# An encoder layer's normalisation stage written out in each engine's order, with B's products ahead and the meta tokens second

## The chip, the cores and the metric

The kernel runs on one core of a Trainium2 chip. TensorE (PE) multiplies matrices; VectorE (DVE), ScalarE (ACT) and GpSimd (POOL) work element by element; SyncE (SP) issues most of the transfers (DMAs). Each of these engines runs its instructions strictly in order, and waits on semaphores for what other engines or transfers have yet to finish. The metric is the time of one launch on the device in microseconds (us), the median of three runs.

## The reference

The reference is one encoder layer in float32 on 512 tokens of 2048 values, with 16 learned meta tokens put ahead of them. Three branches (linear attention, differential attention, a state-space scan) read column groups of one input projection. What the change touches is the start:

```
h = jnp.concatenate([meta, x], axis=1)
u = rmsnorm(h, norm_w)
proj = u @ w_in.astype(dt_)
(gq, gk, gv, ggate, gcode, dq, dk, dv, dgate, z, xbc, dt_raw) = jnp.split(proj, split_idx, axis=-1)
...
dt = jax.nn.softplus(dt_raw.reshape(Bsz, L, 2, SSD_HEADS).astype(jnp.float32) + ssd_dt_bias.astype(jnp.float32))
```

Here rmsnorm divides each token by the root of its mean square and multiplies by norm_w.

## The kernel before

**Blocks.** The tokens lie in blocks of 128: t = 0 to 3 are x's, t = 4 is the 16 meta tokens. The first half of the columns (HA = 272) holds meta and blocks 0 and 1, the second (HB = 256) blocks 2 and 3. The 2048 values of a token are 16 tiles (KT) of 128, called features here and counted by k.

**The stage.** Each block of x is loaded in four tiles of 512 columns (line 86). `normalize` squares each tile with a running sum (ACT line 259, DVE line 262), adds the four sums and EPS (line 264), raises the result to −0.5 on POOL (line 266, "r", called the root here) and scales the tiles with it. `features` transposes 128 x 128 pieces on PE into a PSUM tile "pb" (line 279). ACT copies it, scaled by norm_w, into `uh[k]` (helper line 72), rounded to the part that TensorE takes in one pass. DVE writes what is left into `ul[k]` (line 282).

**The products.** A weight is split in the same way: ACT copies the raw tile "wraw" to "whi" (line 72), DVE subtracts to "wlo". For a column group "B", `t1_half` makes three products per feature: hi·uh, hi·ul, lo·uh (line 39, into a PSUM tile "pm"). For a small group "comb" (gcode and dt_raw, 64 columns whose hi and lo lie side by side) `comb_half` makes two. B's weights come from line 157 and are split in four pieces of 512 columns (line 162), comb's from line 228 in two (line 231). All later weights come through `wsplit` (load line 141, split line 146), in pieces of 1024 columns, under a high priority. Its raw tiles "wraw" share two buffers with B's.

**After the stage.** The first half of B is copied to "xp" (ACT), comb is transposed and goes into "dts", "dtt" and, with exp of A_log ("ea", line 358), into "at" (line 360).

**What sets the order.** The program is written block after block, and a scheduler in the framework decides where each instruction stands on its engine, by its own estimates. Semaphores are placed after that. The semaphores of SP's and ACT's transfers are eight, DMAHW0 to DMAHW7, used in turn: a transfer is issued only when the one that had the same semaphore eight issues earlier has landed. The small vectors come by lines 116 to 119, the meta tokens by line 107, the identity matrix that the transposes use by line 112, the norm weights "gn" of two branches by lines 304 and 305, scaled at once by lines 306 and 307.

Of the kernel before, what the change touches and what calls it, by code (L numbers as in the profile page):

```python
# [42 lines left out]
def encoder_kernel(ctx, tc, x, meta, rel_bias, final_norm_w, norm_w, w_in, w_out, gla_wa2, gla_ba,  # L43
                   gla_norm_w, diff_lambda, diff_norm_w, conv_w, conv_b, A_log, dt_bias, ssd_D,
                   ssd_norm_w, masks, umask, onehot, out):
    nc = tc.nc
# [36 lines left out]
    def load_x(t):
        for j in range(4):
            xt[t, j] = slot("ya" if t < 2 else "o", [P, 512], name="xt")
            nc.sync.dma_start(xt[t, j], xv[t][:, j * 512:(j + 1) * 512])

    warm = const.tile([P, 1], F32, name="warm")
    nc.vector.memset(warm, 0.0)
    nc.scalar.activation(warm, warm, AF.Exp)  # L90
# [34 lines left out]

# [26 lines left out]
    def t1_weights(c0, nk, tag):  # L152

        out_ = []
        for k0 in range(0, KT, 8):
            raw = wpool.tile([P, 8, P], F32, name="wraw")
            nc.sync.dma_start(raw, win[:, k0:k0 + 8, c0:c0 + P])
            for i in range(0, 8, nk):
                hi = slot(tag, [P, nk, P], F32R, name="whi")
                lo = slot(tag, [P, nk, P], F32R, name="wlo")  # L160
                cpy(hi, raw[:, i:i + nk])
                tt(lo, raw[:, i:i + nk], hi.bitcast(F32), ALU.subtract)
                out_.append((hi, lo))
        return out_

    def t1_half(acc, ws, hf):
        nk = KT // len(ws)
        o, us = (acc[0][:, 0:HA], slice(0, HA)) if hf == 0 else (acc[1][:, 0:HB], slice(HA, L))
        for k in range(KT):
            hi, lo = ws[k // nk]  # L170
            for n, (wt, ur) in enumerate(((hi, uh[k]), (hi, ul[k]), (lo, uh[k]))):
                mm(nc, o, wt[:, k % nk, :], ur[:, us], k == 0 and n == 0, k == KT - 1 and n == 2)
# [61 lines left out]
    load_x(2)  # L234
    load_x(3)

    def comb_half(acc, hf):

        o, us = (acc[0][:, 0:HA], slice(0, HA)) if hf == 0 else (acc[1][:, 0:HB], slice(HA, L))
        for k in range(KT):  # L240
            for n, ur in enumerate((uh[k], ul[k])):
                mm(nc, o, comb_w[k // 8][:, k % 8, :], ur[:, us], k == 0 and n == 0, k == KT - 1 and n == 1)

    vt = const.tile([P, 92], F32, name="vt")
    pv = pb()
    nc.tensor.transpose(pv[:, 0:92], vecs, ident[0:92, 0:92])
    nc.vector.tensor_copy(vt, pv[:, 0:92])
    nw = vt[:, 0:16]
    gba = vt[:, 88:92]

    def normalize(t):
        rows = NM if t == 4 else P
        ss = small.tile([P, 1], F32, name="ss")
        ssq = small.tile([P, 5], F32, name="ssq", bufs=5)
        nc.gpsimd.memset(ssq[:, 4:5], EPS)
        for j in range(4):
            scr = slot("w")
            if j < (2 if t < 2 else 3):
                nc.scalar.activation(scr[0:rows, 0:512], xt[t, j][0:rows], AF.Square, scale=D ** -0.5,
                                     accum_out=ssq[0:rows, j:j + 1])  # L260
            else:
                nc.vector.tensor_tensor_reduce(scr[0:rows, 0:512], xt[t, j][0:rows], xt[t, j][0:rows], 1.0 / D, 0.0,
                                               ALU.mult, ALU.add, ssq[0:rows, j:j + 1])
        nc.vector.tensor_reduce(ss[0:rows], ssq[0:rows], AX.X, ALU.add)
        r = small.tile([P, 1], F32, name="r")
        gtt(r[0:rows], ss[0:rows], mhalf[0:rows, 0:1], ALU.pow)
        for j in range(4):
            if j == 3:
                cpy(xt[t, j][0:rows], xt[t, j][0:rows], scale=r[0:rows, 0:1])
            else:  # L270
                ts_(xt[t, j][0:rows], xt[t, j][0:rows], r[0:rows, 0:1], None, ALU.mult)

    def features(parts, us):
        for k in range(KT):
            pt = pb()
            n = 0
            for t in parts:

                nc.tensor.transpose(pt[:, n:n + P], xt[t, k // 4][:, (k % 4) * P:(k % 4 + 1) * P], ident)
                n += NM if t == 4 else P  # L280
            cpy(uh[k][:, us], pt[:, 0:n], scale=nw[:, k:k + 1])
            stt(ul[k][:, us], pt[:, 0:n], nw[:, k:k + 1], uh[k][:, us].bitcast(F32), ALU.mult, ALU.subtract)
# [20 lines left out]
    gn = const.tile([P, 2, P], F32, name="gn")  # L303
    nc.sync.dma_start(gn[:, 0], gla_norm_w.broadcast_to([P, P]))
    nc.sync.dma_start(gn[:, 1], diff_norm_w.broadcast_to([P, P]))
    ts_(gn[:, 0], gn[:, 0], 0.5, None, ALU.mult)
    ts_(gn[:, 1], gn[:, 1], 1.0 - LAMBDA_INIT, 0.5, ALU.mult, ALU.mult)
# [701 lines left out]
```

## Time and profile before

| What | Value |
|---|---|
| Time, median of 3 runs | 900.89 us (899.99 to 901.36) |
| The profiled execution's own time | 897.21 us |
| Span of its records | 895.3 us |
| TensorE busy | 865.2 us, 97% of the span |
| VectorE, ScalarE, GpSimd busy | 536.1, 419.8, 142.2 us |

The span is what the profiler's records cover; the profiled execution's own time has 1.9 us around it. The rows below are times of that one execution, counted from the start of the span.

### The profile page before, as it was taken

What the parts mean: (1) busy time and instruction counts of PE and PEld (TensorE: products, weight loads), DVE (VectorE), ACT (ScalarE), POOL (GpSimd) and SP (SyncE); (2) the same over time, 40 slices, a digit from 0 to 9 for tenths busy, and PEclk for the clock granted to TensorE, in tenths of its full rate; (3) what the DMA queues carried; (4) which work ended last, traced back from release to release, by engine and by line L of the source; (5) the groups of instructions that cost most, each with busy time, mean ns of one, the idle gap of its engine ahead of it and who ended that gap; (6) DMA issues with size and microseconds to landing.
All of it is one profiled execution on the core that took longest, in us unless ns stands there. A gap on an engine that the chain in (4) does not pass through costs nothing.

```text
span 895.3 us, 14457 instructions
## 1 busy us (share of the span) xinstructions
PE 865.2 (97%) x5705; PEld 772.8 (86%) x5705; DVE 536.1 (60%) x1035; ACT 419.8 (47%) x828; POOL 142.2 (16%) x185
## 2 busy tenths in 40 slices
PE   3999989999999999999999999999999999999996
PEld 3999989998888899999999999988888888888884
DVE  6655897998977787944532577665552633232333
ACT  7667945439743487543222364543431432231322
POOL 2000004640335302000330000100110002020200
PEclk9999999999999999999999999999999999999998
DMA  9534731244523233222355322243223532222225
GB/s 240 135 94 129 205 94 49 71 119 142 158 78 94 72 94 95 72 71 72 90 148 141 95 75 82 86 118 116 71 84 96 169 133 94 94 94 95 82 83 188
DMA packets 104116, 96.77 MB, mean 108 GB/s; under 512 B 8624, under 2 KB 75816, under 8 KB 104048
## 3 DMA queue, kind: packets, MB, share of 16 engines
q1 hardware_dynamic: 99647, 85.43, 34.0%
q0 software_dynamic: 1520, 5.17, 2.0%
q10 hardware_dynamic: 2880, 5.24, 1.8%
q8 instruction: 45, 0.74, 0.3%
q14 instruction: 24, 0.19, 0.1%
HBM read 91.55 MB, written 6.41 MB: 109 GB/s over the span
## 4 chain that ended last, share of the span: by engine, by line
PE 76%; DVE 9%; ACT 5%; DMA 5%; issue 3%; SPq 1%; POOL 0%; ACTq 0%; POOLq 0%; DVEq 0%
PE pm L39 65%; PE pb L39 8%; DVE acc L410 2%; DMA xt<-in_x_dram 2%; ACT dtm L437 1%; DVE wlo L146 1%; DVE sg L446 1%; DMA sb<-xd 1%; ACT sg L445 1%; PE pb L894 1%; PE pb L848 1%; DVE m L551 1%; DMA sg<-xd 1%; ACT whi L72 1%; DMA wraw<-in_w_in_dram 1%
## 5 line engine op out<-in xcount | busy, mean ns | idle before, releaser
L146 DVE TENSOR_TENSOR wlo<-wraw,whi 128x1024 fp32r<-128x1024 f32 (+1 forms) x128 | 160.2, 1251 | 192.1 <-ACT whi L72 191.9
L72 ACT ACTIVATE whi<-wraw 128x1024 fp32r<-128x1024 f32 (+1 forms) x134 | 137.3, 1025 | 270.3 <-PE pm L39 214.5
L39 PE MATMUL pm<-uh,whi 128*128 128x272 f32 (+2 forms) x960 | 223.7, 298 | 2.6 <-ACT xp L72 2.6
L39 PE MATMUL pm<-ul,whi 128*128 128x272 f32 (+2 forms) x960 | 226.1, 299 | 0.0
L39 PE MATMUL pm<-uh,wlo 128*128 128x272 f32 (+2 forms) x928 | 216.5, 297 | 0.0
L39 PEld LDWEIGHTS pm<-uh,whi 128*128 128x128 f32 x960 | 155.4, 189 | 7.9 <-ACT xp L72 2.8
L39 PEld LDWEIGHTS pm<-ul,whi 128*128 128x128 f32 x960 | 155.4, 189 | 4.9 <-issue 0.4
L39 PEld LDWEIGHTS pm<-uh,wlo 128*128 128x128 f32 x928 | 150.1, 189 | 4.5
L39 PE MATMUL pm<-whi,mh 128*128 128x512 f32 x256 | 100.9, 394 | 0.4 <-ACT mh L72 0.4
L39 PE MATMUL pm<-whi,ml 128*128 128x512 f32 x256 | 101.0, 396 | 0.0
L39 PE MATMUL pm<-wlo,mh 128*128 128x512 f32 x256 | 100.9, 394 | 0.0
L39 PE MATMUL pm<-wlo,uh 128*128 128x512 f32 x256 | 100.9, 394 | 0.0
L39 PE MATMUL pm<-whi,ul 128*128 128x512 f32 x256 | 100.8, 395 | 0.0
L39 PE MATMUL pm<-whi,uh 128*128 128x512 f32 x256 | 100.1, 397 | 0.0
L129 POOL TENSOR_TENSOR rs_r<-rs_v,mhalf 128x1 f32<-128x1 f32 (+1 forms) x28 | 20.6, 737 | 266.1 <-DVE rs_v L128 194.1
L39 PEld LDWEIGHTS pm<-whi,mh 128*128 128x128 f32 x256 | 48.1, 188 | 11.6 <-ACT mh L72 0.6
L39 PEld LDWEIGHTS pm<-wlo,mh 128*128 128x128 f32 x256 | 48.1, 188 | 11.2
L39 PEld LDWEIGHTS pm<-whi,ul 128*128 128x128 f32 x256 | 48.1, 188 | 11.0
L39 PEld LDWEIGHTS pm<-whi,ml 128*128 128x128 f32 x256 | 48.0, 188 | 11.0
L39 PEld LDWEIGHTS pm<-wlo,uh 128*128 128x128 f32 x256 | 48.2, 188 | 10.5
L39 PEld LDWEIGHTS pm<-whi,uh 128*128 128x128 f32 x256 | 48.1, 188 | 10.4
L928 POOL TENSOR_TENSOR hx<-hx,fw 128x512 f32<-128x512 f32 x12 | 18.1, 1543 | 164.9 <-ACT junk L915 164.9
(299 smaller groups left out, 1160.7 us busy)
## 6 DMA issues: line engine op xcount, KB each, us to landing
wraw<-in_w_in_dram SPq DMA_DIRECT2D x96, 512.0 KB, 3.9
wraw<-in_w_out_dram SPq DMA_DIRECT2D x30, 512.0 KB, 3.6
xt<-in_x_dram SPq DMA_DIRECT2D x16, 256.0 KB, 4.9
sg<-xd SPq DMA_DIRECT2D x16, 256.0 KB, 4.4
sb<-xd SPq DMA_DIRECT2D x16, 256.0 KB, 4.8
hx<-in_x_dram ACTq DMA_DIRECT2D x16, 256.0 KB, 3.7
out_dram<-hx SPq DMA_DIRECT2D x16, 256.0 KB, 2.9
tabr<-tabd POOLq DMA_DIRECT2D x4, 520.0 KB, 6.9
```

The lines of the kernel that those rows point to most:

```text
L39: nc.tensor.matmul(out, lhsT=lhsT, rhs=rhs, start=start, stop=stop)
L72: nc.scalar.activation(out, in_, AF.Copy, **kw)
L129: gtt(r[0:rows, 0:cols], v[0:rows, 0:cols], mhalf[0:rows, 0:cols], ALU.pow)
L146: tt(lo, raw, hi.bitcast(F32), ALU.subtract)
L410: stt(acc, xp[:, k:k + L], cw[:, k:k + 1], acc, ALU.mult, ALU.add)
L437: nc.scalar.activation(dtm[:, c], mtile[:, M_LE, :], AF.Identity, scale=dtd[:, c, h:h + 1], bias=dtt[:, c, 16 + h:17 + h])
L445: nc.scalar.activation(sg[:, c], sg[:, c], AF.Identity, bias=Xs[:, 0, c, h:h + 1])
L446: stt(sg[:, c], sb[:, c], Xs[:, 1, c, h:h + 1], sg[:, c], ALU.subtract, ALU.min)
L551: tt(m, m, sc, ALU.mult)
L848: nc.tensor.transpose(pt[:, c * P:(c + 1) * P], w_[:, c * P:(c + 1) * P], ident)
L894: nc.tensor.transpose(pt[:, c * P:(c + 1) * P], src[:, j * P:(j + 1) * P], ident)
L928: gtt(hx[t, b], hx[t, b], fw[b], ALU.mult)
```

## The change

The whole stage is written out by hand, in the order in which each engine is to run it, inside `tc.manual_schedule()`, which leaves each engine's instructions in program order. The functions `load_x`, `t1_weights`, `comb_half`, `normalize` and `features` become smaller steps, and a loop over the features calls them. Block 0 is squared first, then the meta tokens, then block 1; block 1's root stands ahead of the meta tokens'. The identity and the meta tokens (now four transfers) are issued from ACT's queue, the small vectors from POOL's. The first half's loop makes B's products feature by feature, and those of comb 12 features later; two of 28 other steps (`todo`) stand behind each feature. The loads of block 2 come ahead of comb's weights. gn's load and scaling are written much later in the program, and "ea" keeps its place in the program's order.

```diff
@@ the start: loads, tiles, splits are taken out of their old places @@
-    for i in range(2):
-        mt = wpool.tile([P, 1024], F32, name="mt", tag="whi" if i else "wlo", bufs=3)
-        nc.gpsimd.memset(mt, 0.0)
-        nc.sync.dma_start(mt[0:NM], meta[:, i * 1024:(i + 1) * 1024])
...
-    for t in (4, 0, 1):
-        normalize(t)
-    features((4, 0, 1), slice(0, HA))
-    comb_ps, b_ps = (pm(), pm()), (pm(), pm())
-    t1_half(b_ps, b_w, 0)
-    comb_half(comb_ps, 0)
-    for t in (2, 3):
-        normalize(t)
-    features((2, 3), slice(HA, L))
-    t1_half(b_ps, b_w, 1)
-    comb_half(comb_ps, 1)
...
+    def turn(hf, k, parts):
+
+        if (hf, k) not in pts:
+            pts[hf, k] = pb()
+        n = 0
+        for t in BL[hf]:
+            if t in parts:
+
+                nc.tensor.transpose(pts[hf, k][:, n:n + P], xt[t, k // 4][:, (k % 4) * P:(k % 4 + 1) * P], ident)
+            n += NM if t == 4 else P
...
+    with tc.manual_schedule():
+
+        load_x(0)
+        nc.scalar.dma_start(ident, masks[M_ID])
+        nc.vector.memset(warm, 0.0)
+        nc.scalar.activation(warm, warm, AF.Exp)
+        for j in range(4):
+            xt[4, j] = slot("ya", [P, 512], name="mt")
+            nc.vector.memset(xt[4, j], 0.0)
+            nc.scalar.dma_start(xt[4, j][0:NM], meta[:, j * 512:(j + 1) * 512])
+        nc.vector.memset(zp, 0.0)
+        nc.gpsimd.memset(mhalf, -0.5)
+        load_x(1)
...
+        load_b()
+        load_b()
+        load_x(2)
+        load_comb()
+        load_comb()
+        load_x(3)
+        cpy(XE, zp[0:96, 0:8].rearrange("p a b -> p (a b)"))
+        cpy(BE, vz[0][0:96])
+        cpy(RB, vz[0][0:96, 0:4])
+
+        square(0, 0, "A")
+        square(0, 2, "V")
+        square(0, 1, "A")
+        square(0, 3, "V")
+        root(0)
...
+        for j in range(4):
+            square(4, j, "A")
...
+        square(1, 2, "V")
+        square(1, 0, "A")
+        square(1, 3, "V")
+        square(1, 1, "A")
+        root(1)
+        root(4)
+        scale(4, 0, "V")
+        scale(0, 1, "A")
+        split_b()
+        LEAD = 3
...
+        CLAG = 12
+        for k in range(KT + CLAG):
+            if k < KT:
+                parts_of_u(0, k)
+                if k + LEAD < KT:
+                    turn(0, k + LEAD, BL[0])
+                prod_b(0, k)
+            for _ in range(2):
+                if todo:
+                    todo.pop(0)()
+            if k >= CLAG:
+                prod_comb(0, k - CLAG)
+            if k >= KT + CLAG - LEAD:
+                turn(1, k - (KT + CLAG - LEAD), BL[1])
         for k in range(KT):
...
+            parts_of_u(1, k)
+            if k + LEAD < KT:
+                turn(1, k + LEAD, BL[1])
+            prod_b(1, k)
+            if k >= 1:
+                prod_comb(1, k - 1)
+        prod_comb(1, KT - 1)
...
-    nc.scalar.activation(ea, row32[:, 32:64], AF.Exp)
+    tc.keep_in_program_order(nc.scalar.activation(ea, row32[:, 32:64], AF.Exp))
...
+    nc.sync.dma_start(gn[:, 0], gla_norm_w.broadcast_to([P, P]))
+    nc.sync.dma_start(gn[:, 1], diff_norm_w.broadcast_to([P, P]))
+    tc.keep_in_program_order(ts_(gn[:, 0], gn[:, 0], 0.5, None, ALU.mult))
+    tc.keep_in_program_order(ts_(gn[:, 1], gn[:, 1], 1.0 - LAMBDA_INIT, 0.5, ALU.mult, ALU.mult))
```

What this makes of the engines' order is shown at three places. First the start of ACT, before; a row is a line, an operation, output<-input and size, and in brackets the semaphores that it waits for (DMAHW3 and so on are landings of transfers).

```order
L90 ACTIVATE warm<-warm 128x1 [waits DVE_49]
L72 ACTIVATE XE<-zp 96x512 [waits DVE_49]
L72 ACTIVATE BE<-zp 96x128
L72 ACTIVATE RB<-zp 96x4
L259 ACTIVATE w,ssq<-mt 16x512 [waits DMAHW3_49,Pool_49]
L259 ACTIVATE w,ssq<-mt 16x512
L259 ACTIVATE w,ssq<-mt 16x512 [waits DMAHW4_49,Pool_49]
L259 ACTIVATE w,ssq<-xt 128x512 [waits DMAHW0_49]
```

The same place after:

```order
L279 ACTIVATE warm<-warm 128x1 [waits DVE_49]
L283 DMA mt<-in_meta_tokens_dram 16x512 [waits DVE_49]
L283 DMA mt<-in_meta_tokens_dram 16x512 [waits DMAHW0_49,DVE_49]
L283 DMA mt<-in_meta_tokens_dram 16x512 [waits DMAHW2_49,DVE_49]
L283 DMA mt<-in_meta_tokens_dram 16x512 [waits DMAHW4_49,DVE_49]
L72 ACTIVATE XE<-zp 96x512 [waits DVE_49]
L72 ACTIVATE BE<-zp 96x128
L72 ACTIVATE RB<-zp 96x4
L186 ACTIVATE w,ssq<-xt 128x512 [waits DMAHW1_49]
L186 ACTIVATE w,ssq<-xt 128x512
```

Four issues now stand ahead of ACT's first copy and first square. DMAHW0 is here the landing of the identity, DMAHW1 to DMAHW4 those of block 0's four tiles.

Second, DVE around the first weight split of 1024 columns, before; ul_136 to ul_151 are the first half's ul of k = 0 to 15.

```order
L282 SCALAR_TENSOR_TENSOR ul_148<-pb,vt,uh_132 128x272
L282 SCALAR_TENSOR_TENSOR ul_149<-pb,vt,uh_133 128x272
L282 SCALAR_TENSOR_TENSOR ul_150<-pb,vt,uh_134 128x272
L146 TENSOR_TENSOR wlo<-wraw,whi 128x1024
L282 SCALAR_TENSOR_TENSOR ul_151<-pb,vt,uh_135 128x272
```

After, ul_99 to ul_114 are k = 0 to 15, and line 116 is the split:

```order
L259 SCALAR_TENSOR_TENSOR ul_108<-pb,vt,uh_92 128x272
L236 TENSOR_TENSOR whi<-wraw,whi 128x8x64
L116 TENSOR_TENSOR wlo<-wraw,whi 128x1024
L259 SCALAR_TENSOR_TENSOR ul_109<-pb,vt,uh_93 128x272
L189 ISA w,ssq<-xt 128x512
L189 ISA ssq 128x1
L259 SCALAR_TENSOR_TENSOR ul_110<-pb,vt,uh_94 128x272
L189 ISA w,ssq<-xt 128x512
L189 ISA ssq 128x1
L195 TENSOR_REDUCE ss<-ssq 128x1
L259 SCALAR_TENSOR_TENSOR ul_111<-pb,vt,uh_95 128x272
L205 TENSOR_SCALAR xt<-xt,r 128x512 x2
```

The split has moved from behind k = 14 to behind k = 9, and block 3's squares and scales from ahead of it to behind it. On ACT its copy stands likewise, behind uh of k = 9.

Third, PE at the last features of the first half, before (uh_135 and ul_151 are k = 15; 128x272 is the first half of the tokens, 128x256 the second):

```order
L39 MATMUL pm<-uh_135,whi 128x272 x2
L39 MATMUL pm<-uh_120,whi 128x256 x2
L39 MATMUL pm<-ul_151,whi 128x272
L39 MATMUL pm<-uh_135,wlo 128x272
L39 MATMUL pm<-ul_151,whi 128x272
```

After (uh_98 and ul_114 are k = 15):

```order
L39 MATMUL pm<-uh_98,whi 128x272
L39 MATMUL pm<-ul_114,whi 128x272
L39 MATMUL pm<-uh_98,wlo 128x272
L39 MATMUL pm<-uh_86,whi 128x272
L39 MATMUL pm<-ul_102,whi 128x272
L39 MATMUL pm<-uh_87,whi 128x272
L39 MATMUL pm<-ul_103,whi 128x272
```

Before, comb's products of a feature follow B's at once, and products of the second half have begun by then; after, comb's of k = 3 to 15 stand behind B's last.

## Rows read from the trace of the kernel before

**Rows 1.** The page: TensorE's busy time, share of the span and instructions.
```profile
PE 865.2 (97%) x5705; PEld 772.8 (86%) x5705; DVE 536.1 (60%) x1035; ACT 419.8 (47%) x828; POOL 142.2 (16%) x185
```

**Rows 2.** Windows of four stretches: busy time by engine, clock, DMA share, GB/s.
```profile
0.00:11.58 11.58, 0.00 (x0) 0.03 (x1) 4.59 (x14) 6.96 (x21) 4.40 (x18) 1.00 0.81 238
11.58:29.67 18.09, 14.13 (x80) 12.22 (x80) 14.49 (x44) 14.49 (x35) 2.35 (x7) 1.00 1.02 220
29.67:71.00 41.33, 41.33 (x345) 41.31 (x346) 27.38 (x53) 25.65 (x45) 0.45 (x5) 1.00 0.36 92
140.00:200.00 60.00, 58.60 (x536) 56.03 (x535) 57.00 (x61) 25.87 (x43) 30.31 (x30) 1.00 0.30 80
```

**Rows 3.** Waits of PE: its line, what released it, total, times, longest.
```profile
PE pm L39 <- ACT xp L72: 2.6, 1, 2.6
```

**Rows 4.** Timeline of PE: products at 21 us, transposes, the last low product.
```profile
21.13 0.43 PE L39 MATMUL pm<-uh,whi 128*128 128x272 f32 x1
21.35 0.43 PE L39 MATMUL pm<-ul,whi 128*128 128x272 f32 x1
...
29.67 0.33 PE L279 MATMUL pb<-masks,mt 128*128 128x128 f32 x1 [1.76 <-DVE ul L282]
...
31.64 0.27 PE L279 MATMUL pb<-masks,mt 128*128 128x128 f32 x1
...
36.44 0.29 PE L39 MATMUL pm<-uh,wlo 128*128 128x272 f32 x1
```

**Rows 5.** Chain (start, us), SP's issues, landings of lines 157 and 141.
```profile
1.17 4.37 DMA xt<-in_x_dram
...
23.92 4.97 DMA gn<-in_diff_norm_w_dram
...
6.63 0.33 SPq L86 DMA_DIRECT2D xt<-in_x_dram  x1
...
25.34 1.01 SPq L141 DMA_DIRECT2D wraw<-in_w_in_dram  x2
...
DMA to landing us min/median/max: 4.0/4.8/5.5
...
DMA to landing us min/median/max: 7.0/7.0/7.0
```

**Rows 6.** Timeline of ACT: start, us, line, operation, out<-in, count, wait.
```profile
2.13 0.61 ACT L72 ACTIVATE XE<-zp 96x512 fp32r<-96x512 f32 x1
...
2.85 0.19 ACT L72 ACTIVATE RB<-zp 96x4 fp32r<-96x4 f32 x1
...
8.77 0.61 ACT L259 ACTIVATE w<-xt 128x512 f32<-128x512 f32 x1
...
9.38 0.61 ACT L259 ACTIVATE w<-xt 128x512 f32<-128x512 f32 x1
...
16.08 0.49 ACT L72 ACTIVATE uh<-pb,vt 128x272 fp32r<-128x272 f32 x1
...
32.95 1.06 ACT L72 ACTIVATE whi<-wraw 128x1024 fp32r<-128x1024 f32 x1 [0.30 <-PE pb L279]
```

**Rows 7.** Timeline of POOL: the root for block 1.
```profile
14.24 0.56 POOL L266 TENSOR_TENSOR r<-ss,mhalf 128x1 f32<-128x1 f32 x1 [1.92 <-DVE ss L264]
```

**Rows 8.** Timeline of DVE: feature parts, splits, gn, scales.
```profile
17.43 0.49 DVE L282 SCALAR_TENSOR_TENSOR ul<-pb,vt,uh 128x272 fp32r<-128x272 f32 x1
17.84 0.67 DVE L162 TENSOR_TENSOR wlo<-wraw,whi 128x512 fp32r<-128x512 f32 x1
18.44 0.49 DVE L282 SCALAR_TENSOR_TENSOR ul<-pb,vt,uh 128x272 fp32r<-128x272 f32 x1
...
28.91 0.23 DVE L307 TENSOR_SCALAR gn<-gn 128x128 f32<-128x128 f32 x1 [2.09 <-DMA gn<-in_diff_norm_w_dram]
...
30.34 1.27 DVE L271 TENSOR_SCALAR xt<-xt,r 128x512 f32<-128x512 f32 x3
...
34.04 1.23 DVE L146 TENSOR_TENSOR wlo<-wraw,whi 128x1024 fp32r<-128x1024 f32 x1 [0.79 <-ACT whi L72]
```

More of the change, by code (lines that the diff above doesn't have):

```diff
@@ L81, in encoder_kernel @@
     xt = {}
[L83 to L90, printed above, removed]
     zp = const.tile([P, 15, 64], F32, name="zp")
-    nc.vector.memset(zp, 0.0)
     vz = [zp[:, 2 * i:2 * i + 2].rearrange("p a b -> p (a b)") for i in range(4)]
@@ L150, in encoder_kernel @@
     wout = w_out.rearrange("o (k p) c -> p (o k) c", p=P)
[L152 to L172, printed above, removed]
     def t1(cols, tokens=True):
@@ L220, in encoder_kernel, with load_x @@
     ul = [upool.tile([P, L], F32R, name=f"ul{k}", tag=f"ul{k}") for k in range(KT)]
-    b_w = t1_weights(C_B, 4, "st")
-    comb_w = []
-    for k0 in (0, 8):
+    mtile = const.tile([P, 5, P], F32, name="masks")
+    ident = mtile[:, M_ID, :]
+    vt = const.tile([P, 92], F32, name="vt")
+    nw = vt[:, 0:16]
+    gba = vt[:, 88:92]
+    warm = const.tile([P, 1], F32, name="warm")
+    ssq, rx = {}, {}
+    def load_x(t):
+        for j in range(4):
+            xt[t, j] = slot("ya" if t < 2 else "o", [P, 512], name="xt")
+            nc.sync.dma_start(xt[t, j], xv[t][:, j * 512:(j + 1) * 512])
@@ new lines, in square, with root @@
+    def square(t, j, eng):
+        rows = NM if t == 4 else P
+        scr = slot("w")
+        if eng == "A":
+            nc.scalar.activation(scr[0:rows, 0:512], xt[t, j][0:rows], AF.Square, scale=D ** -0.5,
+                                 accum_out=ssq[t][0:rows, j:j + 1])
+        else:
+            nc.vector.tensor_tensor_reduce(scr[0:rows, 0:512], xt[t, j][0:rows], xt[t, j][0:rows], 1.0 / D, 0.0,
+                                           ALU.mult, ALU.add, ssq[t][0:rows, j:j + 1])
+    def root(t):
+        rows = NM if t == 4 else P
+        ss = small.tile([P, 1], F32, name="ss")
+        nc.vector.tensor_reduce(ss[0:rows], ssq[t][0:rows], AX.X, ALU.add)
+        rx[t] = small.tile([P, 1], F32, name="r")
+        gtt(rx[t][0:rows], ss[0:rows], mhalf[0:rows, 0:1], ALU.pow)
@@ new lines, in scale, with load_b, split_b @@
+    def scale(t, j, eng):
+        rows = NM if t == 4 else P
+        ap = xt[t, j][0:rows]
+        if eng == "A":
+            cpy(ap, ap, scale=rx[t][0:rows, 0:1])
+        else:
+            ts_(ap, ap, rx[t][0:rows, 0:1], None, ALU.mult)
+    b_raw, b_w, comb_raw, comb_w = [], [], [], []
+    def load_b():
+        raw = wpool.tile([P, 8, P], F32, name="wraw")
+        k0 = 8 * len(b_raw)
+        nc.sync.dma_start(raw, win[:, k0:k0 + 8, C_B:C_B + P])
+        b_raw.append(raw)
+    def split_b():
+        n = len(b_w)
+        raw = b_raw[n // 2][:, 4 * (n % 2):4 * (n % 2) + 4]
+        hi = slot("st", [P, 4, P], F32R, name="whi")
+        lo = slot("st", [P, 4, P], F32R, name="wlo")
+        cpy(hi, raw)
+        tt(lo, raw, hi.bitcast(F32), ALU.subtract)
+        b_w.append((hi, lo))
@@ L226, in encoder_kernel, with load_comb, split_comb @@
+    def load_comb():
         raw = slot("ev", [P, 8, 64], name="wraw")
+        k0 = 8 * len(comb_raw)
         for i, c0 in enumerate((C_CODE, C_DT)):
             nc.sync.dma_start(raw[:, :, 32 * i:32 * i + 32], win[:, k0:k0 + 8, c0:c0 + 32])
+        comb_raw.append(raw)
+    def split_comb():
+        raw = comb_raw[len(comb_w)]
         w_ = wpool.tile([P, 8, P], F32R, name="whi", bufs=3)
@@ L232, in encoder_kernel @@
         comb_w.append(w_)
[L234 to L239, printed above, removed]
-        for k in range(KT):
[L241 to L282, printed above, removed]
-    for t in (4, 0, 1):
-        normalize(t)
@@ new lines, in parts_of_u, with prod_b @@
+    def parts_of_u(hf, k):
+        us, n = US[hf], (HA, HB)[hf]
+        pt = pts[hf, k]
+        cpy(uh[k][:, us], pt[:, 0:n], scale=nw[:, k:k + 1])
+        stt(ul[k][:, us], pt[:, 0:n], nw[:, k:k + 1], uh[k][:, us].bitcast(F32), ALU.mult, ALU.subtract)
+    def prod_b(hf, k):
+        o = b_ps[hf][:, 0:(HA, HB)[hf]]
+        hi, lo = b_w[k // 4]
+        for n, (wt, ur) in enumerate(((hi, uh[k]), (hi, ul[k]), (lo, uh[k]))):
+            mm(nc, o, wt[:, k % 4, :], ur[:, US[hf]], k == 0 and n == 0, k == KT - 1 and n == 2)
@@ new lines, in prod_comb @@
+    def prod_comb(hf, k):
+        o = comb_ps[hf][:, 0:(HA, HB)[hf]]
+        for n, ur in enumerate((uh[k], ul[k])):
+            mm(nc, o, comb_w[k // 8][:, k % 8, :], ur[:, US[hf]], k == 0 and n == 0, k == KT - 1 and n == 1)
+    vecs = slot("st", [92, P], name="vecs")
+    with tc.manual_schedule():
[10 more added lines that the diff above has]
+        load_x(1)
+        for t in range(5):
+            ssq[t] = small.tile([P, 5], F32, name="ssq", bufs=5)
+            nc.gpsimd.memset(ssq[t][:, 4:5], EPS)
+        nc.gpsimd.dma_start(vecs[0:16], norm_w.rearrange("o (k p) -> (o k) p", p=P))
+        nc.gpsimd.dma_start(vecs[16:76], conv_w.rearrange("o k (j p) -> (o k j) p", p=P))
+        nc.gpsimd.dma_start(vecs[76:88], conv_b.rearrange("o (j p) -> (o j) p", p=P))
+        nc.gpsimd.dma_start(vecs[88:92].rearrange("h (z k) -> h z k", z=2),
+                            gla_ba.rearrange("o z (h k) -> (o h) z k", h=4))
+        load_b()
[12 more added lines that the diff above has]
+        root(0)
+        pv = pb()
+        nc.tensor.transpose(pv[:, 0:92], vecs, ident[0:92, 0:92])
+        for j in range(4):
+            square(4, j, "A")
+        nc.vector.tensor_copy(vt, pv[:, 0:92])
+        scale(0, 0, "V")
+        scale(0, 2, "V")
+        square(1, 2, "V")
[8 more added lines that the diff above has]
+        LEAD = 3
+        for k in range(LEAD):
+            turn(0, k, (4, 0))
+        scale(1, 0, "V")
+        scale(1, 1, "A")
+        scale(4, 1, "V")
+        for k in range(LEAD):
+            turn(0, k, (1,))
+        todo = [lambda: split_b(), lambda: scale(1, 2, "V"), lambda: scale(4, 2, "V"), lambda: scale(0, 3, "A"),
+                lambda: scale(1, 3, "A"), lambda: scale(4, 3, "V"),
+                lambda: split_b(), lambda: square(2, 0, "A"), lambda: square(2, 2, "V"), lambda: square(2, 1, "A"),
+                lambda: square(2, 3, "V"), lambda: split_comb(), lambda: root(2), lambda: split_b(),
+                lambda: scale(2, 0, "V"), lambda: scale(2, 1, "V"), lambda: scale(2, 2, "V"), lambda: scale(2, 3, "A"),
+                lambda: split_comb(), lambda: square(3, 0, "A"),
+                lambda: square(3, 2, "V"), lambda: square(3, 1, "A"), lambda: square(3, 3, "V"),
+                lambda: root(3), lambda: scale(3, 0, "V"), lambda: scale(3, 1, "V"),
+                lambda: scale(3, 2, "V"), lambda: scale(3, 3, "A")]
+        CLAG = 12
[12 more added lines that the diff above has]
+                turn(1, k - (KT + CLAG - LEAD), BL[1])
+        for k in range(KT):
+            parts_of_u(1, k)
[5 more added lines that the diff above has]
+        prod_comb(1, KT - 1)
@@ L302, in encoder_kernel @@
     nc.sync.dma_start(row32[:, 64:80], ssd_D.broadcast_to([P, 16]))
[L303 to L307, printed above, removed]
     nc.sync.dma_start(mtile[:, 1:5], masks[1:5].rearrange("m p q -> p m q"))
@@ L757, in encoder_kernel @@
     gla_pair(1, gla_pair(0, dd))
+    gn = const.tile([P, 2, P], F32, name="gn")
+    nc.sync.dma_start(gn[:, 0], gla_norm_w.broadcast_to([P, P]))
+    nc.sync.dma_start(gn[:, 1], diff_norm_w.broadcast_to([P, P]))
+    tc.keep_in_program_order(ts_(gn[:, 0], gn[:, 0], 0.5, None, ALU.mult))
+    tc.keep_in_program_order(ts_(gn[:, 1], gn[:, 1], 1.0 - LAMBDA_INIT, 0.5, ALU.mult, ALU.mult))
     rb = small.tile([32, 4], F32, name="rb")
```

21 lines of the change are left out of this document (4 added, 17 removed).

## The prediction

> **What bounds the kernel now.** I read the page first: TensorE (PE) is busy for 865.2 us, 97% of the span [rows 1]. A change in this stage therefore acts in two ways only: it moves the moment from which PE is never short of input, and it changes how many of PE's 5705 instructions are done by then. Next I read the windows [rows 2]: PE does nothing until 11.58, is busy 14.13 of 18.09 us up to 29.67, and 41.33 of 41.33 us from there to 71. So in the kernel before, the stage hands over at 29.67; what is late at that point is late at the end, unless a later wait of PE soaks it up. The waits name one of some size, 2.6 us for ScalarE's copy to xp [rows 3]. The timelines of PE, DVE, ACT, POOL and SP give the prices.
>
> Two PE rows serve as marks. The first half's last product with the low part of B's weights starts at 36.44 [rows 4]; it is the 137th PE instruction before and the 104th after (counted in the order of instructions). Between 29.67 and 31.64 stand 16 PE instructions, 0.123 us each [rows 4].
>
> **The change, part by part.**
>
> *The start (ACT's queue).* Before, SP issues the meta transfers, and ACT waits for data only. After, ACT issues the identity and four meta transfers, and the second to fourth carry waits for landings, the last for the fourth tile of block 0 (DMAHW4 in the order). ACT runs in order, so its three copies and all its squares stand behind that. Tiles of x landed at 5.54 (1.17 + 4.37) and by 6.63 (SP's issue that waits for it) [rows 5], 1.1 us apart, so the fourth lands at 7.3 to 7.7. With 0.45 us for the issue and 0.9 us for the copies (2.13 to 3.04 [rows 6]) the first square starts near 8.7. Two squares of block 0, four of meta and two of block 1 follow at 0.61 each (8.77 to 9.38 [rows 6]), 4.9 us, so the sums are there near 13.8. Block 1's root comes first, then meta's: two pows at 0.56 [rows 7] and a reduce make 15.3; meta's scale on DVE makes 15.7. Three blocks' transposes and one copy: the first uh (high part of a feature) near 17.5, where before has 16.08 [rows 6], and the first ul (low part) near 18.0 against 17.43 [rows 8]. The stage starts 0.6 us later, not earlier. If ACT were not held, the squares could start at 5, but block 1's tiles would still decide.
>
> The Trainium skill ("DMA: Bandwidth & Descriptors", section "Issuing engines are not separate DMA queues") says that transfers started by different engines share the same 16 DMA engines, so that spreading them saves sequencer time alone. The trace agrees that the DMAs are the limit here: their share is 0.81 up to 11.58 and 1.02 up to 29.67 [rows 2]. By the rule the moved issues bring next to nothing; by the row they free seven issues of some 0.33 us on SP [rows 5], 2.3 us, which bring something only where SP, and not a landing, is late. With the rule alone, W below would stay at its upper bound and the sum at +7.9.
>
> *The first half's loop (DVE).* After the first ul, DVE has: 16 ul at 0.41 (17.43 to 17.84) = 6.5; five splits of 512 columns at 0.60 (17.84 to 18.44) = 3.0; four squares at 0.61, taken as ACT's [rows 6], = 2.4; nine scales at 0.40 (1.27 for three) = 3.6; one split of 1024 columns and two reduces, 1.3 [rows 8]. That is 16.8 us, so 34.8 at the earliest for the last ul, and 35.8 with the wait for block 3's root. This is a floor.
>
> *The first ordinary weights (ACT and DVE).* Their 1024-column split stands between the 10th and 11th features on both engines after, and between the 15th and 16th before. Nothing behind it on ACT or DVE runs until its load has landed, at W. Behind it stand, on DVE: ACT's copy 1.06 [rows 6], the split 1.2, six ul 2.45, two squares 1.22, three scales 1.2 [rows 8], a reduce and block 3's pow 0.6 [rows 7], and hand-overs 0.3: 8.0 us. So the last product of B in the first half stands at T = W + 8.0, or at the floor if that is later.
>
> *W.* SP issues this load behind block 3 of x, the masks and gn, as before. Before, that was at 25.34, and it landed 7.0 us later, at 32.3; B's loads took 4.8 at the median, and just ahead gn's transfer took 4.97 [rows 5]. After, the issue can be up to 2.3 us earlier (seven issues of 0.33 us leave SP [rows 5]) or as late as before, because the bytes ahead of it are the same. Bounds: 23.0 + 4.8 = 27.8 and 25.34 + 7.0 = 32.3. Between them I take 30.0, the middle, because gn and the crowded DMAs stay. T = 38.0 (35.8 and 40.3 at the ends, the lower one by the floor).
>
> *gn.* Before, DVE waits 2.09 us for gn, and PE then 1.76 us [rows 4, 8]. After, the scaling stands much later; that gain is inside T. Two operations of 0.2 us are moved to a place where DVE has room. If DVE still waited there: 2.1 us on DVE, not on PE.
>
> *The products left over.* At its mark, PE has done 33 instructions fewer than before (137 − 104): nearly all of the small "comb" products lag by 12 features. From there PE is fed without a break in both programs. 33 × 0.123 = 4.0 us.
>
> *Sum.* Delay = T + 4.0 − 36.44 = 38.0 + 4.0 − 36.44 = **+5.6 us**; with the ends of W +3.4 and +7.9. One more wait is possible: the product that needs dt's decay ("at") stands 11 instructions nearer to the transposes of comb, 1.4 us at most; I put it at nothing, as PE has 93 instructions of 0.12 us between. From about 180 us on PE's order is the same. The profiled execution would be 897.2 + 5.6 = 902.8; the median shown, 900.89, is 3.7 above that profiled time, so the median would be **906.5**.
>
> **Rivals.**
>
> *No change that shows.* The delay is soaked up later: by the 2.6 us at xp [rows 3] and the 1.4 us that PE idles between 140 and 200 (60.00 − 58.60 [rows 2]). 5.6 − 4.0 = +1.6, about 902.5. For it: these waits are on ACT and DVE, which run ahead while PE is late. Against it: their inputs are PE's own products, equally late.
>
> *Faster.* The order of features works as written: ACT's squares are not held, block 1's last tile lands by 10.7, and with a square, pow, scale and transposes the first ul is there at 13.0 instead of 18.0; the weights land early too. Then T is the floor, 13.0 + 16.8 = 29.8, and 29.8 + 4.0 − 36.44 = −2.6: 898.3. It decides where the first ul comes before 13.8 and W before 22.6 (T + 4.0 below 34.6, that is 1.8 us gained). Against it: ACT's waits in the order, and the load issued behind block 3 of x, whose landing ended SP's waits at 25.3 before [rows 5].
>
> *Slower still.* PE's products start 0.22 us apart at 21.13 and 21.35, and 0.123 after 29.67 [rows 4], while the clock column reads 1.00 (2.4 GHz) in both stretches [rows 2]; so early work goes at about half pace whatever the column says. In the new loop PE needs six instructions for each feature, 1.35 us at the slow pace, where DVE gives a feature each 1.05 us (16.8 / 16). If the slow pace lasts for half of the 16, that is 8 × 0.35 = 2.8 us more: 909.3. Against it: before, PE had gone to the quick pace and kept it through 1.76 us of idling. The Trainium skill ("TensorE: Matmul & The Clock Gate", section "HAM oscillation") says that a loop whose matmuls wait again and again for their input falls back to the slower clock each time; by it this case would come about, and PE's waiting loop is just such a one.
>
> **How the numbers follow.** About 0.2% (1.8 us) is what a measurement of this kernel can tell from no change. My forecast holds 0.63 (904.3 to 908.8, the ends of W), the slower rival 0.14, the soaked-up delay 0.14 and the faster one 0.09. Slower by over 0.2%: 0.63 + 0.14 and no part of the rest, 0.77; within: 0.14; faster: 0.09. The range leaves out the faster case and the far half of the slower: 901.4 to 909.8.
>
> **What would show it.** Right: ACT's first square near 8.7, not 6.9; the first ul at 17.5 to 18.5; ACT idle between the 10th feature and the 1024-column copy, which starts at W, near 30; the last B product at 38; PE then 4 us of comb products without a pause; the wait for gn gone from DVE. Wrong: a first square before 7.5, a W below 26, or PE's wait at xp gone by the time PE gets there.

## The result, and the profile after

The changed kernel takes 905.18 us (median of 5, 904.29 to 905.52), the kernel before 900.76 (median of 5, 898.02 to 901.36). The ratio is 1.0064, 95% interval 1.0047 to 1.008: slower by 4 to 7 us; the two medians alone give 1.0049. Its profiled execution took 904.29 us, with a span of 902.5; the one of before had 897.21 and 895.3. That profile of before is quicker than any of its five timed runs, so the two profiles stand 7.1 us apart and the medians 4.4.

The page of after, engine by engine; beside [rows 1], TensorE's busy time is 2.4 us up for the same 5705 instructions:

```profile
PE 867.6 (96%) x5705; PEld 775.1 (86%) x5705; DVE 539.2 (60%) x1040; ACT 419.4 (46%) x827; POOL 140.6 (16%) x187
```

Windows of after (stretch, length, busy us of PE, PEld, DVE, ACT, POOL, granted clock, DMA share, GB/s):

```profile
0.00:11.58 11.58, 0.39 (x1) 0.18 (x1) 5.54 (x18) 5.11 (x14) 4.64 (x21) 1.00 0.84 247
11.58:29.67 18.09, 12.71 (x72) 11.38 (x72) 14.90 (x38) 13.72 (x34) 2.17 (x4) 1.00 0.97 220
29.67:71.00 41.33, 37.15 (x289) 36.70 (x289) 23.19 (x45) 21.75 (x44) 0.77 (x5) 0.92 0.29 76
```

In the third row PE is busy 37.15 of 41.33 us and does 289 instructions, where before it was busy throughout and did 345 [rows 2]: 56 instructions fewer, against 7 fewer up to 29.67. Most of the loss lies here, not at the start. The waits of PE name it, with the one at xp below:

```profile
PE pm L39 <- ACT uh L72: 4.1, 1, 4.1
PE pm L39 <- ACT xp L72: 2.1, 1, 2.1
```

The timeline of ACT (start, us, engine, line, operation, in brackets the idle time ahead and what ended it) shows why no uh came:

```profile
4.57 3.33 ACTq L283 DMA_DIRECT2D mt<-in_meta_tokens_dram  x3
7.95 0.63 ACT L72 ACTIVATE XE<-zp 96x512 fp32r<-96x512 f32 x1 [5.29 <-DMA xt<-in_x_dram]
...
8.78 0.61 ACT L186 ACTIVATE w<-xt 128x512 f32<-128x512 f32 x1
...
17.60 0.49 ACT L72 ACTIVATE uh<-pb,vt 128x272 fp32r<-128x272 f32 x1 [1.94 <-PE pb L252]
...
31.74 1.06 ACT L72 ACTIVATE whi<-wraw 128x1024 fp32r<-128x1024 f32 x1 [3.37 <-DMA wraw<-in_w_in_dram]
```

First the hold at the start, 5.29 us for block 0's last tile; then 3.37 us for the first ordinary weights. DVE stands in the same place:

```profile
18.12 0.50 DVE L259 SCALAR_TENSOR_TENSOR ul<-pb,vt,uh 128x272 fp32r<-128x272 f32 x1 [0.98 <-ACT uh L72]
...
32.83 1.23 DVE L116 TENSOR_TENSOR wlo<-wraw,whi 128x1024 fp32r<-128x1024 f32 x1 [3.38 <-ACT whi L72]
```

PE's timeline, from the pause to the last low product of the first half (40.03, against 36.44 in [rows 4]):

```profile
33.83 0.59 PE L39 MATMUL pm<-uh,whi 128*128 128x272 f32 x1 [4.08 <-ACT uh L72]
...
38.23 0.43 PE L39 MATMUL pm<-uh,whi 128*128 128x272 f32 x1
38.46 0.42 PE L39 MATMUL pm<-ul,whi 128*128 128x272 f32 x1
38.71 0.29 PE L39 MATMUL pm<-uh,wlo 128*128 128x272 f32 x1
38.84 0.29 PE L39 MATMUL pm<-uh,whi 128*128 128x272 f32 x1
...
40.03 0.28 PE L39 MATMUL pm<-uh,wlo 128*128 128x272 f32 x1
```

Behind the pause the products start 0.23 us apart, from 38.7 on 0.13.

**A mark for the stage.** Executions differ later on by a microsecond or two, so I compare the stage by one PE instruction that stands at the same place in all kernels, the one with number 700 in the order of starts (733 in a_fill, which has 33 more ahead). It starts at 104.61 before and at 112.29 after, 7.7 us later (PE's timeline of before, then that of after):

```profile
104.61 0.41 PE L39 MATMUL pm<-uh,whi 128*128 128x272 f32 x2
```

```profile
112.29 0.41 PE L39 MATMUL pm<-uh,whi 128*128 128x272 f32 x2
```

From number 300 to number 850 the distance to the kernel before changes by 0.6 us at most in every kernel (by 0.4 in after), so the mark does not hang on the number chosen. But each mark comes from one execution, and the start alone differs from one to the next: in the seven kernels whose starts are written alike (after, a_gnlate, a_split, a_clag6, a_fill, a_split_clag6, a_split_clag6_gnlate) ACT's first square is at 8.17 to 8.78 and the first uh at 16.94 to 17.60. Differences of up to half a microsecond between two marks need a second look.

All marks, as time behind the kernel before, with the ratio of the timed runs:

| Kernel | Mark | Ratio (95% interval) |
|---|---|---|
| after | +7.7 | 1.0064 (1.0047 to 1.008) |
| a_gnlate | +5.0 | 1.0041 (1.0026 to 1.0056) |
| a_split | +3.3 | 1.0016 (1.0006 to 1.0027) |
| a_clag6 | +7.5 | 1.0051 (1.0036 to 1.0066) |
| a_actfree | +8.6 | 1.007 (1.0056 to 1.0085) |
| a_fill | +7.3 | 1.0069 (1.0054 to 1.0084) |
| a_split_clag6 | +1.6 | 1.0032 (1.002 to 1.0044) |
| a_split_clag6_meta | +2.2 | 1.0017 (1.0004 to 1.0031) |
| a_split_clag6_gnlate | +1.5 | 1.0009 (0.9997 to 1.0021) |
| a_start | +0.4 | 0.9979 (0.9968 to 0.9989) |
| b_gnlate | −1.6 | 0.9969 (0.9959 to 0.998) |

### The profile page after: what moved, and what is told of

The parts are those of the page before. It is cut to its first block, busy times and chain, and to the rows that moved or that the text cites. A ratio compares the mean times of both kernels' runs of the same rounds, so it can differ in the third digit from the quotient of the medians.

```text
span 902.5 us, 14460 instructions
## 1 busy us (share of the span) xinstructions
PE 867.6 (96%) x5705; PEld 775.1 (86%) x5705; DVE 539.2 (60%) x1040; ACT 419.4 (46%) x827; POOL 140.6 (16%) x187
## 4 chain that ended last, share of the span: by engine, by line
PE 82%; DVE 8%; ACT 3%; DMA 3%; issue 2%; SPq 1%; ACTq 0%; POOLq 0%; POOL 0%; DVEq 0%
PE pm L39 70%; PE pb L39 8%; DVE wlo L116 1%; DVE acc L474 1%; DMA xt<-in_x_dram 1%; DVE sg L510 1%; DMA wraw<-in_w_in_dram 1%; DMA sb<-xd 1%; PE pb L964 1%; PE pb L918 1%; SPq L180 1%; ACT dtm L501 1%; DVE Ss L519 1%; SPq L229 1%; PE pb L252 1%
## 5 line engine op out<-in xcount | busy, mean ns | idle before, releaser
L116 DVE TENSOR_TENSOR wlo<-wraw,whi 128x1024 fp32r<-128x1024 f32 (+1 forms) x128 | 162.5, 1269 | 194.7 <-ACT whi L72 189.1
L39 PE MATMUL pm<-uh,whi 128*128 128x272 f32 (+2 forms) x960 | 227.1, 300 | 6.2 <-ACT uh L72 4.1
L39 PE MATMUL pm<-uh,wlo 128*128 128x256 f32 (+2 forms) x928 | 216.7, 298 | 0.0
L39 PEld LDWEIGHTS pm<-uh,whi 128*128 128x128 f32 x960 | 156.6, 189 | 11.6 <-ACT uh L72 4.3
L39 PEld LDWEIGHTS pm<-whi,mh 128*128 128x128 f32 x256 | 48.1, 188 | 11.6 <-ACT mh L72 0.6
```

Source lines behind the costliest of these rows:

```text
L116: tt(lo, raw, hi.bitcast(F32), ALU.subtract)
```

## The experiments

Theory W says that the first ordinary weights, whose split stands behind feature 9, hold ACT and DVE until they land, at W. Its rivals: S, the stage is late because it starts late; C, TensorE's slow pace behind its pause is what costs.

**1. gn's transfers out of the way (a_gnlate).** The orders of PE, DVE, ACT and POOL are those of after; only SP's differs.

```diff
-    nc.sync.dma_start(gn[:, 0], gla_norm_w.broadcast_to([P, P]))
-    nc.sync.dma_start(gn[:, 1], diff_norm_w.broadcast_to([P, P]))
+    tc.keep_in_program_order(nc.sync.dma_start(gn[:, 0], gla_norm_w.broadcast_to([P, P])))
+    tc.keep_in_program_order(nc.sync.dma_start(gn[:, 1], diff_norm_w.broadcast_to([P, P])))
```

> The changed kernel with gn's two transfers kept behind all earlier transfers of SP in the program, so that they are issued far later and no longer ahead of the first ordinary weights. Theory W (ACT and DVE are held until the first ordinary weights land): in the trace of after, gn's two transfers of 64 KB land 3.45 us after the transfer ahead of them (26.56 to 30.01) and the weights 1.71 us later, at 31.72; without them W comes near 28.3, ACT's idle time ahead of its 1024-column copy falls from 3.4 to under 0.5 us, the last low product of B's first half from 40.0 to about 36.7, and the span from 902.5 to about 899.1. Theory S (the stage is late because it starts late: first uh at 17.6 in place of 16.1): span within 0.5 of 902.5. Theory C (only TensorE's slow pace behind its 4.1 us pause costs): 1 to 2 us gained, 900.5 to 901.5.

ACT's timeline in a_gnlate:

```profile
29.01 1.06 ACT L72 ACTIVATE whi<-wraw 128x1024 fp32r<-128x1024 f32 x1 [0.83 <-DMA wraw<-in_w_in_dram]
```

W is 2.7 us earlier (31.74 to 29.01), and the mark 2.7 (7.7 to 5.0): the stage follows W one to one. The gain is less than the 3.3 expected, because W fell to 29.0 and not to 28.3; the transfer ahead of the weights landed at 27.35 there, 0.8 us later than in after. The span, 901.0, fell by 1.5 alone; the granted clock of this execution is 0.86 at 128 to 140, where after has 1.00. Windows of after show what gn does to the transfers: at 26 to 28, with the two gn transfers of 64 KB at the head of the line, the DMAs are busy for 0.77 of the time and move 46 GB/s.

```profile
26.00:28.00 2.00, 1.65 (x12) 1.24 (x10) 1.96 (x6) 1.25 (x3) 0.90 (x2) 1.00 0.77 46
28.00:30.00 2.00, 1.65 (x11) 1.38 (x11) 1.45 (x4) 0.37 (x1) 0.00 (x0) 1.00 1.03 219
```

The same stretch of a_gnlate, without them:

```profile
26.00:28.00 2.00, 1.55 (x12) 1.14 (x10) 1.97 (x6) 1.44 (x3) 0.70 (x2) 1.00 1.02 281
```

**2. The split away from feature 9 (a_split).** The first split is bound, on both engines, behind feature 2 of the second half.

```diff
         with tc.high_priority():
-            cpy(hi, raw)
-            tt(lo, raw, hi.bitcast(F32), ALU.subtract)
+            split = cpy(hi, raw), tt(lo, raw, hi.bitcast(F32), ALU.subtract)
+        if behind:
+            for ins, name in zip(split, behind.pop()):
+                tc.add_manual_dep(ins.ins, name, NOSYNC, reason="behind")
...
+        if (hf, k) == (1, 2):
+            behind.append((a.ins.name, v.ins.name))
```

> The changed kernel with the split of the first ordinary weights moved on ACT and DVE from behind feature 9 of the first half to behind feature 2 of the second half; transfers as they were. Theory W: neither engine waits at feature 9, block 3's squares follow at once, the last low product stands near 35.7 in place of 40.0, PE has no pause of 4 us, and the span is about 898.2 (4.3 less). The load lands at 31.7 as before. Theory S: span within 0.5 of 902.5. Theory C: 900.5 to 901.5.

The last low product stands at 35.27 in PE's timeline of a_split, and the split runs at 40.34 without a wait (ACT's timeline):

```profile
35.27 0.29 PE L39 MATMUL pm<-uh,wlo 128*128 128x272 f32 x1
```

```profile
40.34 1.05 ACT L72 ACTIVATE whi<-wraw 128x1024 fp32r<-128x1024 f32 x1
```

The mark gains 4.4 us, the span 4.8 (897.7), as W says; the first uh is at 17.40, as late as in after. S and C fall for this part.

**3. PE kept busy in its pause (a_fill).**

```diff
                     turn(0, k + LEAD, BL[0])
+                if k == 9:
+                    for _ in range(11):
+                        turn(0, k + LEAD, BL[0])
                 prod_b(0, k)
```

> The changed kernel with 33 transposes of feature 12 done again on PE at feature 9, some 3.7 us of work in the pause of 4.1 us that PE spends there. Theory W (the load holds ACT and DVE; PE's slow pace behind the pause lies under DVE's features, one each 0.9 us): PE's products start 0.125 us apart behind the pause in place of 0.23, but the last low product moves by 0.4 us at most (40.0 to 39.6), and the span by less than 0.5 from 902.5. Theory C (the slow pace from 33.8 to 38.5 is what costs): 4.7 us at half pace, 2.3 us gained, span near 900.2.

Windows of after, and then those of a_fill, for the stretch behind the pause (the third number from the end is the granted clock):

```profile
30.00:32.00 2.00, 0.00 (x0) 0.00 (x0) 0.00 (x0) 0.26 (x1) 0.00 (x0) 0.95 0.99 273
32.00:34.00 2.00, 0.17 (x1) 0.17 (x1) 1.17 (x2) 2.00 (x5) 0.00 (x0) 0.50 0.16 43
34.00:36.00 2.00, 1.91 (x7) 1.60 (x8) 2.00 (x6) 1.52 (x5) 0.00 (x0) 0.50 0.36 52
36.00:38.00 2.00, 2.00 (x10) 2.00 (x10) 1.64 (x7) 0.98 (x2) 0.63 (x3) 0.50 1.14 324
38.00:40.00 2.00, 2.00 (x14) 1.95 (x14) 1.53 (x4) 0.49 (x2) 0.00 (x0) 0.84 0.11 25
```

```profile
32.00:34.00 2.00, 1.21 (x8) 0.76 (x7) 1.64 (x3) 2.00 (x7) 0.00 (x0) 1.00 0.02 6
34.00:36.00 2.00, 1.90 (x12) 1.53 (x12) 1.97 (x7) 1.05 (x3) 0.03 (x1) 1.00 0.63 148
36.00:38.00 2.00, 1.04 (x7) 0.77 (x6) 1.68 (x5) 1.45 (x3) 0.60 (x3) 1.00 0.86 245
```

The slow level (0.50, 1.2 GHz) is gone in a_fill, and PE then waits for DVE: busy 1.04 of 2 us at 36 to 38. The mark gains 0.4 us and the span 0.4, but this is not the price of the clock: in this execution the weights landed 0.5 us earlier. ACT's copy and PE's last low product in a_fill, then that product in a_gnlate:

```profile
31.27 1.06 ACT L72 ACTIVATE whi<-wraw 128x1024 fp32r<-128x1024 f32 x1 [3.34 <-DMA wraw<-in_w_in_dram]
...
39.57 0.29 PE L39 MATMUL pm<-uh,wlo 128*128 128x272 f32 x1
```

```profile
37.30 0.29 PE L39 MATMUL pm<-uh,wlo 128*128 128x272 f32 x1
```

From the copy to that product are 8.30 us in a_fill, 8.29 in after (31.74 to 40.03) and 8.29 in a_gnlate (29.01 to 37.30); from there to the mark a_fill and after both take 72.3. So the slow stretch is real, but in after it cost nothing that these rows can tell: it lay under DVE's work. The timed ratio, 1.0069, is no lower than that of after. C falls.

**4. Comb's products earlier, with the wait left in (a_clag6).**

```diff
-        CLAG = 12
+        CLAG = 6
```

> The changed kernel with comb's products 6 features behind B's in place of 12. By the prediction's term of the products left over, 12 to 14 of 33 products are done before the mark: 1.5 to 1.7 us gained if PE has room there. But from 33.8 PE goes at the slow pace without a gap until 38.5, so that only the 8 products of features 0 to 3, which now stand ahead of the pause, find room: 8 x 0.123 = 1.0 us, span about 901.5. The last low product itself stands later than 40.0. Theory S: 902.5.

A miss: the mark gained 0.2 and not 1.0. Part of that is W, which came 0.5 us later in this execution; counted from W the gain is 0.7. PE's timeline has the last low product at 41.33, and PE's clock is at 0.50 from 34 to 40 there. Of the 18 comb products that now stand ahead of it, 8 come before the pause and 10 behind it, in the slow stretch. ACT's copy and that product in a_clag6:

```profile
32.23 1.06 ACT L72 ACTIVATE whi<-wraw 128x1024 fp32r<-128x1024 f32 x1 [4.19 <-DMA wraw<-in_w_in_dram]
...
41.33 0.29 PE L39 MATMUL pm<-uh,wlo 128*128 128x272 f32 x1
```

**5. The same with the wait taken out (a_split_clag6).** a_split and CLAG = 6 together.

> a_split with comb's products 6 features behind B's in place of 12. PE is now at the quick pace and waits for DVE in each feature, so that the moved products find room: 12 to 14 of the 33 left over, 1.5 to 1.7 us. At PE's 700th instruction a_split stands 3.3 us behind the kernel before; here it would be 1.7. If the late start alone makes up the 3.3 us: no change against a_split.

At the mark 1.6 us behind before, 1.7 less than a_split: the term of the products left over is right once PE has room for them. The timed ratio did not follow (1.0032 against 1.0016, with intervals that overlap). In the profiled execution PE's windows show where it is given back: at 140 to 150 PE waits 1.6 us for DVE's XE, and its granted clock is 0.83, where a_split has 9.27 us busy at 1.00. Windows of a_split_clag6, and then of a_split_clag6_meta (experiment 6):

```profile
140.00:150.00 10.00, 8.35 (x139) 7.93 (x140) 9.93 (x9) 3.91 (x7) 4.13 (x7) 0.83 0.30 82
```

```profile
140.00:150.00 10.00, 8.38 (x162) 7.83 (x161) 9.63 (x8) 4.38 (x7) 4.68 (x7) 1.00 0.29 75
```

The second has the same wait, 1.6 us, but keeps the clock at 1.00 and gets 162 instructions done in place of 139. So the slow clock does not come with the wait alone.

The scheduler's order behind the stage differs between a_split and a_split_clag6 in a few rows of DVE, ACT and PE; which of them makes that wait was not tried.

**6. ACT not held at the start (a_actfree, a_split_clag6_meta, a_start).** Three ways; the third has the small vectors on ACT's queue and the meta tokens on POOL's.

```diff
-            nc.scalar.dma_start(xt[4, j][0:NM], meta[:, j * 512:(j + 1) * 512])
+            nc.gpsimd.dma_start(xt[4, j][0:NM], meta[:, j * 512:(j + 1) * 512])
```

> The changed kernel with the four meta transfers issued by POOL in place of ACT, so that ACT's copies and squares no longer stand behind landings of block 0. Theory W: ACT's first square starts near 5 in place of 8.8 and the first uh 2 to 3 us earlier than 17.6, but the weights still land near 31.7 and hold both engines: span within 0.5 of 902.5, with a longer wait at feature 9. Theory S: the stage and the span gain as much as the first uh, 2 to 3 us: 899.5 to 900.5.

ACT's first square is at 4.92, but the first uh is at 18.19, later than 17.60. POOL issues the small vectors behind the meta tokens; PE's transposition of them waits until 11.6, and DVE, which copies its result in order, squares block 1 that much later. W stays (31.94), the clock is slow until 40.4, and the mark loses 0.9: a miss. Counted from W, the last low product comes 8.98 us later, 0.7 more than in after, though DVE's last ul ends as long after W as there (7.79 us, at 39.73); here the slow stretch outlasts DVE's work, and it does cost.

> a_split_clag6 with the meta transfers issued by SP between blocks 0 and 1, so that ACT is not held at the start. ACT's first square near 5, the first uh near 15 in place of 17.4; with the loop paced by DVE, all of it moves by 2.4 us, and PE's 700th instruction stands at -0.7 us against the kernel before. If the start is not what paces the loop once the weights are out of the way: the same as a_split_clag6.

A miss again: ACT's first square is at 4.92, the first uh at 17.59, and the mark loses 0.6. Now the transfers of block 1 stand behind the meta tokens' on SP, and DVE waits for block 1's last tile (DVE's timeline):

```profile
13.02 0.69 DVE L194 CUSTOM_DVE_ANT_0 w<-xt 128x512 f32<-128x512 f32 x1 [1.61 <-DMA xt<-in_x_dram]
```

So I built a start in which none of the three is late.

> a_split_clag6 with a start in which no engine is held: the small vectors issued by ACT right behind the identity, the meta tokens by POOL. a_actfree and a_split_clag6_meta freed ACT, but the vectors (11.54 against 9.50 us) or block 1's last tile (13.00 against 11.15) landed later and took over the wait. If the start paces the loop, as the sum of the prediction has it: first uh near 15.6 in place of 17.4, and PE's 700th instruction at about -0.2 us against the kernel before (1.65 - 1.8). If block 1's last tile lands after 12.5: no gain.

ACT's timeline in a_start:

```profile
7.22 0.61 ACT L191 ACTIVATE w<-xt 128x512 f32<-128x512 f32 x1
...
16.00 0.49 ACT L72 ACTIVATE uh<-pb,vt 128x272 fp32r<-128x272 f32 x1 [1.95 <-PE pb L257]
```

The first uh comes 1.3 us earlier than in a_split_clag6 (17.27), not 1.8, and the mark gains 1.2 (1.6 to 0.4): ACT's first square, at 7.22, still stands behind the last vectors' issue, which waits for the identity. The forecast of the mark, −0.2, was missed by 0.6. Once the weights are out of the way the start does pace the loop, about one to one. This kernel is faster than the one before, by 0.2% (0.9979).

**7. gn late in two other kernels.** First in a_split_clag6, then in the kernel before:

> a_split_clag6 with gn's transfers late as in a_gnlate. If gn costs the changed kernel only by way of the load on which both engines wait (theory W), nothing is left to gain once that wait is gone: PE's 700th instruction stays at 1.65 us behind the kernel before, within 0.3. If gn's transfer costs the stage in another way too: up to 2.7 us less, as a_gnlate gained.

The mark moved by 0.1: as far as it can tell, gn cost the changed kernel by way of W alone. The timed ratio is lower (1.0009 against 1.0032); the two were timed on different chips, each against the kernel before, and the mark does not explain it.

```diff
-    gn = const.tile([P, 2, P], F32, name="gn")
...
-    ts_(gn[:, 1], gn[:, 1], 1.0 - LAMBDA_INIT, 0.5, ALU.mult, ALU.mult)
...
     gla_pair(1, gla_pair(0, dd))
+    gn = const.tile([P, 2, P], F32, name="gn")
+    tc.keep_in_program_order(nc.sync.dma_start(gn[:, 0], gla_norm_w.broadcast_to([P, P])))
...
```

> The kernel before with gn alone treated as in the change and as in a_gnlate: its load and scaling written behind the linear attention and kept in program order. If gn's transfer is a cost of the kernel before of its own (DVE waits 2.09 us and PE 1.76 us for it): the pause at 27.9 is gone, 1.5 to 1.8 us gained, span near 893.6. If that wait is only covered by a later one: no change.

The pause for gn is gone; the mark is 1.6 us ahead of before. By the profile half of that is given back later (span 894.5 against 895.3), where its granted clock falls. Windows of before, and then of b_gnlate:

```profile
128.00:140.00 12.00, 11.32 (x93) 11.29 (x94) 7.56 (x9) 7.58 (x15) 3.35 (x3) 1.00 0.46 116
```

```profile
128.00:140.00 12.00, 12.00 (x89) 11.92 (x89) 5.96 (x8) 6.12 (x12) 3.40 (x3) 0.86 0.35 90
```

The timed runs give 0.9969, 896.18 us: the lowest ratio of this study, though its interval overlaps that of a_start. It is the one part of the change that was tried alone on the kernel before, and it pays. The run moves the transfer and the scaling together and does not part them. In the kernel before ACT's copy of the weights waited for PE and not for its load (0.30 us [rows 6]), so the gain is more likely DVE's wait for gn than an earlier W.

## Why the prediction was right, point by point

- **The start** was right to 0.1 us: the first square at 8.78 (forecast 8.7), block 1's and meta's roots done at 15.25 (15.3), the first uh at 17.60 (17.5), the first ul at 18.12 (18.0). That it is this close is luck in part, as other executions of the same start have the first uh up to 0.7 us earlier. Experiment 6 adds that the first two ways of freeing ACT made another transfer land later, and so brought nothing.
- **The weights' landing W** was the term that was mis-sized most: 31.7 and not 30.0, inside the bounds 27.8 and 32.3. SP issued the load 1.2 us earlier than before (24.14 against 25.34 [rows 5]), but it took 7.6 us to land. I took the middle of the bounds; the row of before that had gn ahead of the load, 7.0 us, was the nearer one, and gn stands there in after as well.
- **T = W + 8.0** came out as 31.7 + 8.3 = 40.0. The 0.3 is not the slow clock: a_fill, without it, has 8.30. It lies mainly in the hand-overs, put at 0.3 us: DVE's last ul ends 7.79 us behind W (the sum without hand-overs has 7.7), and the product follows 0.50 us later.
- **The floor** of 35.8, set by DVE's work, was met by a_split at 35.3.
- **The 33 products left over**, 4.0 us: 40.0 + 4.0 − 36.4 = 7.6, and the mark says 7.7. a_split_clag6 shows the price again, 1.7 us for the 12 to 14 of them that it moves.
- **gn**: the wait that the kernel before had was worth 1.6 us at the mark (b_gnlate), as its 1.76 us pause said [rows 4]. The changed kernel removes the wait on DVE, but keeps the transfer ahead of the weights, on which ACT and DVE now wait 3.4 us.
- **No wait at "at"**, right; **soaked up later**, wrong as a rival: the wait at xp shrank by 0.5 us alone, from 2.6 [rows 3] to 2.1.
- **The slower rival** was half right. The slow pace did come back, but behind the one pause of 4.1 us and not because of a loop that waits in each feature; DVE's pace covered it, as a_fill shows. The loop's short waits up to 29.67 (0.65 us the longest) left the clock at 1.00, with starts still 0.12 to 0.13 us apart at 29. The Trainium skill ("TensorE: Matmul & The Clock Gate", section "HAM oscillation") has the clock fall, in its example, behind waits for a transfer that are longer than the matmuls between them; the row of 0.50 at 32 to 34, behind the one long wait of this loop, agrees. The rival's own sum has a slip: 1.35 − 1.05 is 0.30 and not 0.35, which makes 2.4 us and 908.9.
- **The total.** Profile against profile the sum gave +5.6 and 7.1 was measured; the difference is W's 1.7, 0.3 of the step to T and 0.5 less waiting at xp. The medians differ by 4.4, 905.18 against the forecast 906.5. That the median came so near is luck in part: W made the delay longer, and the step from the profiled time to the median, which I took as 3.7 us for both kernels, was 0.9 us for the changed one (904.29 to 905.18). The record says something on this step, as it has the mean granted clock of each timed run. Among the 26 runs of the kernel before that were timed beside a_fill, those with 0.997 and 0.998 took 896.35 to 897.52 us, those with 0.993 and 0.994 took 898.55 to 900.93; the profiled execution of before had 0.997. So its short time goes with the clock. Where in the run the clock falls in the longer ones stays open, since there is no second trace of that kernel.

## What to carry to other kernels

When a stage is written out by hand, look at where instructions from outside it (here a prefetch's split under high priority) land in the engines' orders: one that waits for a transfer holds everything behind it, and moving it nine features later was worth 4.4 us at the mark, more than any other single step here. Count what the hand order leaves over when the loop ends, and move it into the loop only where the engine has room. And try the parts alone: the part that paid, taking a small transfer and the scaling that waits for it out of DVE's way, did not need the rest.

## What I had not expected of the hardware

- The two transfers that spread a row of 128 values over 128 partitions, 64 KB each, held the DMAs at 46 GB/s for 2 us, where the stretch behind them had 219, and the same stretch without them 281; without them the 512 KB behind landed 2.7 us earlier.
- At its first work PE goes at half pace (starts 0.22 to 0.23 us apart until 21.5) while the clock column reads 1.00, but behind the pause at 29.7 the column does show 0.50.
- A granted clock below 1.00 also comes up at 128 to 150 us in some executions (0.86 in b_gnlate, 0.83 in a_split_clag6), and the length of the wait ahead does not tell in which. Behind a wait of 2.6 us at xp it fell in b_gnlate and not in before; behind 1.6 us for XE it fell in a_split_clag6 and not in a_split_clag6_meta. In b_gnlate half of what the stage had gained was gone by the end.
